# A hybrid SSD and attention block: short groups of transposes ahead of the quads of the gate and up products

## The chip, the cores and the metric

The kernel runs on one core of one Trainium2 chip. The metric is the time of the whole kernel on the device, in microseconds (us); lower is better.

## The reference

One layer of a streaming-encoder block in float32, for 1024 tokens of width 1024. A Mamba-2 SSD group (8 heads) and a stick-breaking attention group (8 heads) work side by side on one projection, then comes a SwiGLU channel mixer with 2816 hidden channels. Cut to the parts that matter here:

```python
h = rms_norm(x, pre_mix_gain)
proj = h @ w_in
z, xbc, dt_raw, q, k, v = split(proj)
y_ssd = ...   # convolution, SSD scan, gated, normed
y_sb = ...    # stick-breaking attention, normed
mix = concatenate([y_ssd, y_sb]) @ w_out
x = x + rms_norm(mix, post_mix_gain)

h = rms_norm(x, pre_ffn_gain)
f = (silu(h @ w_gate) * (h @ w_up)) @ w_down
x = x + rms_norm(f, post_ffn_gain)
```

## The kernel before

Every product is made from operands that are split into two parts: `hi` is the value rounded to float32r and `lo` is what is left of it. ScalarE makes `hi` and VectorE makes `lo` (`split`, L72 and L73), and three matmuls take the place of one: hi x hi, hi x lo, lo x hi (`mm3`, L76 to L78).

The program goes through these stages: the projection together with attention and SSD (to about 485 us), out_proj with its norms (to about 600 us, where the first products of gate and up already stand between its blocks), gate and up (to 1031 us), and down with the last norm.

Gate and up are multiplied as the seven products of Winograd's form of Strassen's product. The 22 tiles of hidden channels are taken in 11 pairs. For each pair p there is one quad for gate and one for up, and `quad(p, name)` is a generator that makes one of the seven products at a time, in the order of its right operands B11, B21, T2, T3, T1, T4, B22. `step(p)` takes the next product of gate's quad and then the same of up's quad, so PE gets gate 1, up 1, gate 2, up 2 and so on. A product is 4 x 3 = 12 matmuls of 128x512 into one bank of PSUM, and a pair of quads has 14 products, 168 matmuls. In the text below "a quad" means such a pair, and "the third quad" is p = 2. The eight banks are taken in a ring, four by gate (`pag`, `pbg`, `pcg`, `peg`) and four by up, so each quad gets the same bank for the same purpose. The bank `pa` holds the first product, goes on accumulating the second, and is then read by the Silu of `gate` (L1002).

Where the operands lie matters below. A tile pool is put on the left or on the right side of the on-chip memory. The right operands of gate and up (B11, B21, T2, T3 in pool `rpA`, T1, T4, B22 in pool `rpB`) lie on the left. The left operands (`flhi`, `fllo`, pool `fw`) lie on the right, except those of the first two products of the first quad (`eo`, in the e tiles of `fwA`), which lie on the left. In down both operands (`fohi`, `folo`) lie on the right. In out_proj W_out (`woh`, `wol`) lies on the right, and the other operand `yhl` too, but for the blocks 2 and 3, where `out_load` puts `yhl` on the left, in the places of T3.

The left operands are loaded, split and kept five steps ahead by `pump(1 + LOOK)`. In the last quad, the loop also starts the loads and splits of down (`unit`, `prep`).

The identity `ident` (128x128, float32, on the left) is used for the transposes that turn the normed rows in out_proj (L1061: 4 transposes for a half, 8 for a block). The clock of TensorE rises with use: the program makes 12 products of ones at its very start (L104).

Of the kernel before, what the change touches and what calls it, by code (L numbers as in the profile page):

```python
# [34 lines left out]
# what in_proj makes, in order; "ssd" from where on SSD's steps run beside the tiles  # L35
PLAN = ('qkv1', 'x0', 'x1', 'x2', 'x3', 'x4', 'x5', 'qkv2', 'x7', 'x6', 'ssd', 'qkv3', 'z0', 'z1', 'r0', 'z2', 'z3', 'wo', 'l1', 'o0')
# how far attention is where the other stream is 0, 1/8, .. 1 done
PACE = (-0.109, 0.104, 0.264, 0.337, 0.474, 0.601, 0.751, 0.876, 1.027)
A_ALL, F_ALL = 146.4, 259.0
SIDE = 1  # L40
WARM = 12
# [6 lines left out]
def tile_hybrid_block(  # L48
# [15 lines left out]
    """The rows of x and out run backwards in time (row s is token S-1-s), so that every  # L64
    running product over earlier tokens is a forward scan along the free axis."""
# [4 lines left out]
    def split(hi, lo, src):  # L70
        """hi + lo == src, hi and lo each exact in float32r."""
        A.copy(hi, src)  # L72
        V.tensor_tensor(lo, src, f32(hi), ALU.subtract)  # L73
# [6 lines left out]
    # ------------------------------------------------------------------ constants  # L80
# [20 lines left out]
    # TensorE's clock rises with use: products of ones while the first loads run  # L101
# [3 lines left out]
    # tri[s, l] = 1 where s >= l  # L105
    tri = const.tile([P, P], F32, name="tri")
    G.affine_select(tri, ones_f, [[-1, P]], ALU.is_ge, 0.0, base=0, channel_multiplier=1)
    # scan floor: 1 where the key is not strictly before the query, 0 elsewhere
# [3 lines left out]
    # column h is 1 on the 64 partitions of head h of a pair  # L112
# [11 lines left out]
    # DRAM scratch  # L124
# [5 lines left out]
    # means of squares and what they make 1 / rms: even heads, odd heads, SSD groups  # L130
# [8 lines left out]
    # ------------------------------------------------------------------ right side: x * gain and in_proj weights  # L139
# [4 lines left out]
    # the rows' 1 / rms scales columns here, so it is applied to what comes out of in_proj  # L144
# [13 lines left out]
    # sel16 sums the products of the two halves of w2  # L158
# [11 lines left out]
    # columns of w_in in the order of their use; each tile is loaded and split while the one before it  # L170
    # is multiplied
# [5 lines left out]
    def fetch_w(half=None):  # L177
        """The next column tile, or one half of it."""
        if cols:
            name, col = cols[0]  # L180
            w = w_tiles.setdefault(name, [])
            for dh in range(2) if half is None else (half,):
                w.append(load_w_half(col, name, dh))
            if len(w) == 2:
                cols.pop(0)
# [8 lines left out]
    # ------------------------------------------------------------------ pre-mix norm, first products  # L194
# [40 lines left out]
    # ------------------------------------------------------------------ left side: attention, conv and SSD work  # L235
# [20 lines left out]
    def qkv_tiles(j, st):  # L256
        """What takes q, k (each in its two parts) and v of a pair of heads out of PSUM, to DRAM."""

        def store(key, n, i, t):
            nc.sync.dma_start(qkv_d[j][key][i][:, 512 * n : 512 * n + 512], t)  # L260

        def two(key, n, src):
            hi, lo = [t2.tile([P, 512], F32R, tag="t2", name=key + x) for x in "hl"]
            split(hi, lo, src)
            store(key, n, 0, f32(hi))
            store(key, n, 1, f32(lo))

        def evac_q(n, ps, sl):
            two("q", n, ps)
            st["q"] = n == 1  # L270

        def evac_k(n, ps, sl):
            kr = t2.tile([P, 512], F32, tag="t2", name="kr")
            V.tensor_tensor(kr, ps, R_b[:, sl], ALU.mult)
            two("k", n, kr)
            st["k"] = n == 1

        def evac_v(n, ps, sl):
            vr = t2.tile([P, 512], F32, tag="t2", name="vr")
            V.tensor_tensor(vr, ps, R_b[:, sl], ALU.mult)  # L280
            if j == 0:
                v_first.append(vr)
            else:
                store("v", n, 0, vr)
            if n == 1:
                st["v"] = True

        return evac_q, evac_k, evac_v
# [7 lines left out]
    # ------------------------------------------------------------------ dt, decays  # L296
    def dt_stage():
# [18 lines left out]
        # softplus(x) = max(x, 0) + log1p(exp(-|x|)), log1p(e) = 2 atanh(e / (2 + e))  # L316
# [43 lines left out]
        # attention's sigmoids, which need these, wait for the last exponential: ScalarE changes its table once  # L360
# [4 lines left out]
    # ------------------------------------------------------------------ conv tiles  # L365
# [38 lines left out]
    # ------------------------------------------------------------------ SSD  # L404
# [76 lines left out]
    def mean_sq(src, sel, rows, n, cnt, ps=None, start=True, stop=True):  # L481
        """Means of squares over channels, to the rows of ss_d."""
# [32 lines left out]
    # ------------------------------------------------------------------ stick-breaking attention  # L515
    CH = {128: [128], 256: [256], 384: [384], 512: [512], 640: [384, 256], 768: [512, 256], 896: [512, 384], 1024: [512, 512]}

    def prep_head(j, st, h):
        """Keys over both halves of the partitions, the query's high part beside its low part."""
# [29 lines left out]
    def weigh(head, qb):  # L549
        """A key k weighs sigmoid(z_k) * prod_{q < i < k} sigmoid(-z_i)."""  # L550
# [20 lines left out]
    def turn(ws, g, jj):  # L571
        """Weights of 256 queries and 256 keys, keys to the partitions, split."""
# [27 lines left out]
    def attention(st):  # L600
        """All heads, as one stream of small steps: products with the values lag the transposes,
        the next queries' weights run ahead of them."""
# [53 lines left out]
    def merge(ga, gb):  # L656
        """Interleave attention with the other stream, as PACE has it."""
# [47 lines left out]
    # ------------------------------------------------------------------ out_proj: the products  # L705
    # position p of a block of 128 tokens: from here on the last rows come first
# [6 lines left out]
    def bank(name):  # L713
        tag = ("mm", "mm", "z", "z", "o", "px", "px", "px")[ring_i[0] % 8]
        ring_i[0] += 1
        return psum(tag, name)
# [4 lines left out]
    # the channels in the order of their use: attention's first, the SSD's second group last  # L721
    KO = (4, 5, 6, 7, 0, 1, 2, 3)

    def fetch_wo():
        """W_out's rows in the order of their use, and the places of their two parts."""
# [31 lines left out]
    def out_load(p, part):  # L757
        """A block of the mixed channels, scaled by their 1 / rms, split: all but the SSD's second
        group, that group, or all."""
# [89 lines left out]
    # ------------------------------------------------------------------ out_proj, post-mix norm, residual, pre-ffn norm  # L849
    # positions 0 .. 7 of a block of 128 tokens: from here on the last rows come first  # L850
# [3 lines left out]
    def row_rstd(ssq):  # L854
        """-2 (ssq / D + eps) ** -0.5 for [P, 2] partial sums; the gains it multiplies take in the -1 / 2."""
# [15 lines left out]
    # Gate and up as the seven products of Winograd's form of Strassen's product: blocks of 512  # L871
    # tokens, halves of d, and pairs of tiles of f. h2 is the right operand:
    #   [b11 b12; b21 b22], halves of d by halves of the tokens
# [13 lines left out]
    def product(ps, lop, rop, start):  # L887
        """ps = or += the product; a bank that was read goes on accumulating after that."""
        (ah, al), (bh, bl) = lop, rop
        for k in range(4):  # L890
            mm3(ps, ah[:, k, :], al[:, k, :], bh[:, k, :], bl[:, k, :], start and k == 0, k == 3, not start)
# [4 lines left out]
    def quad(p, name):  # L896
        """The 2 x 2 blocks of W^T h from seven products. c11 is left in PSUM."""
        tmp = lambda: gp.tile([P, 512], F32, tag="bt", name="c" + name, bufs=4)
        x = "gu".index(name)
        a = bank("pa" + name)  # L900
        product(a, lops[x], B11, True)
# [31 lines left out]
    def left_gen():  # L933
        """The left operands in the order of their use, gate and up in turn."""
# [51 lines left out]
    def step(p):  # L986
        """The next product of gate's and of up's quad p."""
# [8 lines left out]
    def gate(t):  # L996
        """A block of a from gate's and up's."""
# [8 lines left out]
    # which block of a the products make  # L1006
    where = {1: (0, 0), 4: (1, 1), 5: (1, 0), 6: (0, 1)}

    with es_o:
# [3 lines left out]
        def early_ops():  # L1013
            """The left operands of the first two products."""
# [35 lines left out]
        def out_tail(sb, t):  # L1050
# [20 lines left out]
            # T3 = b22 - b12, T2 = T3 + b11, T1 = b12 - b11, T4 = b21 - T2: its product enters with that sign  # L1071
# [50 lines left out]
        # not the ring's next banks: those hold what waits for the last norm  # L1122
# [7 lines left out]
    # ------------------------------------------------------------------ gate and up  # L1130
# [12 lines left out]
    # Down as seven products too: halves of the tokens, even and odd tiles of f, halves of d.  # L1143
    #   a: [a11 a12; a21 a22], tokens by f; w: [b11 b12; b21 b22], f by d
    # What stays on chip takes the places of what gate and up no longer need, in this order.
# [35 lines left out]
    def prep(i):  # L1181
        """The operands of a step, a product's part of one pair of tiles of f."""
# [60 lines left out]
    # ------------------------------------------------------------------ down, post-ffn norm, residual  # L1243
# [15 lines left out]
    def finish(b, halves, xr):  # L1259
        """halves: the block's two, times the gain."""  # L1260
# [76 lines left out]
def _layout(inputs):  # L1337
    """x backwards in time, plain and transposed; the small parameters side by side, a channel
    (of its tile of 128) to a partition; the large ones as they are."""
# [32 lines left out]
```

## Time and profile before

| | |
|---|---|
| median of 3 runs | 1249.93 us (1248.95 to 1252.76) |
| the profiled execution | span 1249.6 us, 0.3 us under the median |
| PE (matmul) busy | 1204.2 us, 96% |
| VectorE (DVE) busy | 932.1 us, 75% |
| ScalarE (ACT) busy | 587.7 us, 47% |
| GpSimd (POOL) busy | 92.1 us, 7% |
| mean granted TensorE clock | 0.989 |

The span is the time from the first to the last instruction of one profiled execution. Busy times are shares of the span. PE and PEld are the matmuls and the weight loads of TensorE, which overlap. A matmul is shown longer than the distance to the next one's start, because matmuls are pipelined, so the rate is read from the distance between starts. The granted clock is 1.00 at 2.4 GHz and 0.50 at 1.2 GHz.

### The profile page before, as it was taken

Reading aid. Unit: us, or ns where it says so; the run is one execution under the profiler, and the core shown is the slowest. Engines: PE = TensorE matmul, PEld = TensorE weight load, DVE = VectorE, ACT = ScalarE, POOL = GpSimd, SP = SyncE. Lnnn points to the kernel's source line nnn. Section 1 sums busy time; section 2 is a strip of 40 time slices with the busy share of each in tenths; the row PEclk is TensorE's granted clock in tenths of the full one; section 3 lists DMA queues with packets and bytes.
Section 4 is the critical chain, followed back from the end, with each engine's and each line's share of the span. In section 5 each row is a group of like instructions: output and inputs, shape, how many; then the busy total and the mean of one; then the engine's idle time right before and its main releaser. Section 6 shows DMA issues by size and latency. Waiting matters only on the chain.

```text
span 1249.6 us, 16320 instructions
## 1 busy us (share of the span) xinstructions
PE 1204.2 (96%) x5641; PEld 972.0 (78%) x5641; DVE 932.1 (75%) x1461; ACT 587.7 (47%) x1115; POOL 92.1 (7%) x232
## 2 busy tenths in 40 slices
PE   8998999999999998998799999999999999999997
PEld 7776778787887776787678888888888888888885
DVE  7478988778997887676897565566555558998777
ACT  7347655556655666444653332333233325444543
POOL 0041110010110100011200000000000000000000
PEclk9998999999999999999899999999999999999999
DMA  5693252445466326754872212312132198133336
GB/s 188 194 358 107 67 152 82 142 117 178 142 181 190 118 93 212 228 173 159 271 207 93 93 60 93 101 59 93 52 100 98 58 327 318 62 124 101 102 135 235
DMA packets 139882, 183.23 MB, mean 147 GB/s; under 512 B 10660, under 2 KB 94852, under 8 KB 139800
## 3 DMA queue, kind: packets, MB, share of 16 engines
q1 hardware_dynamic: 128544, 151.18, 38.3%
q0 software_dynamic: 7424, 25.17, 5.5%
q10 hardware_dynamic: 3832, 5.84, 1.3%
q8 instruction: 44, 0.72, 0.2%
q14 instruction: 38, 0.31, 0.1%
HBM read 132.23 MB, written 49.92 MB: 146 GB/s over the span
## 4 chain that ended last, share of the span: by engine, by line
PE 69%; DVE 14%; DMA 8%; issue 4%; ACT 4%; SPq 2%; DVEq 0%; ACTq 0%
PE pd L77 5%; PE pd L76 5%; PE pd L78 5%; DVE sn L567 3%; DMA Rb<-r_d 3%; PE o L590 2%; PE tp L578 2%; PE pj_x L76 2%; PE pj_x L78 2%; PE pcg L76 2%; PE pj_x L77 2%; PE pcu L76 2%; PE peg L76 2%; PE peu L76 2%; PE peu L77 2%
## 5 line engine op out<-in xcount | busy, mean ns | idle before, releaser
L72 ACT CAST flhi<-fraw 128x512 fp32r<-128x512 f32 x102 | 62.7, 622 | 174.1 <-PE pcg L77 37.0
L77 PE MATMUL pd<-folo,fohi 128*128 128x512 f32 x260 | 101.2, 389 | 0.0
L76 PE MATMUL pd<-fohi 128*128 128x512 f32 x260 | 101.2, 389 | 0.0
L78 PE MATMUL pd<-fohi,folo 128*128 128x512 f32 x260 | 101.1, 389 | 0.0
L567 DVE TENSOR_TENSOR_SCAN sn<-sn,smask 128x1024 f32<-128x1024 f32 (+3 forms) x64 | 87.4, 1366 | 17.7 <-ACT sn L563 17.7
L73 DVE TENSOR_TENSOR fllo<-fraw,flhi 128x512 fp32r<-128x512 f32 x102 | 69.6, 686 | 38.9 <-ACT flhi L72 38.5
L72 ACT CAST fohi<-rt 128x512 fp32r<-128x512 f32 x83 | 48.9, 618 | 51.2 <-PE pd L77 30.7
L563 ACT ACTIVATE sn<-zp,msc 128x512 f32<-128x512 f32 (+2 forms) x96 | 56.0, 585 | 34.3 <-PE zp L562 30.6
L582 ACT CAST wh<-tp 128x512 fp32r<-128x512 f32 (+1 forms) x80 | 42.7, 545 | 38.4 <-PE tp L578 37.9
L72 ACT CAST flhi<-fs 128x512 fp32r<-128x512 f32 x44 | 27.2, 622 | 70.4 <-PE peg L77 37.0
L73 DVE TENSOR_TENSOR folo<-rt,fohi 128x512 fp32r<-128x512 f32 x83 | 55.2, 694 | 6.4 <-ACT fohi L72 6.4
L583 DVE TENSOR_TENSOR wl<-tp,wh 128x512 fp32r<-128x512 f32 (+1 forms) x80 | 49.7, 628 | 10.8 <-ACT wh L582 10.3
L564 ACT ACTIVATE sp<-zp,msc 128x512 f32<-128x512 f32 (+2 forms) x96 | 55.8, 584 | 2.5 <-PE tp L578 2.5
L76 PEld LDWEIGHTS pd<-fohi 128*128 128x128 f32 x260 | 48.8, 188 | 10.3
L78 PEld LDWEIGHTS pd<-fohi,folo 128*128 128x128 f32 x260 | 48.8, 188 | 10.1
L77 PEld LDWEIGHTS pd<-folo,fohi 128*128 128x128 f32 x260 | 48.8, 188 | 10.1
L1004 POOL DMA_DIRECT2D a_d<-sg x44 | 23.7, 540 | 392.4 <-DVE sg L1003 392.4
L76 PE MATMUL pj_x<-hh,wh_x 128*128 128x512 f32 x128 | 52.5, 410 | 0.0
L578 PE MATMUL tp<-ident,sp 128*128 128x128 f32 x288 | 47.6, 276 | 5.0 <-DVE sp L568 4.5
L76 PE MATMUL po<-woh,yhl 128*128 128x512 f32 x128 | 51.0, 399 | 1.0 <-ACT yhl L72 1.0
L78 PE MATMUL po<-woh,yhl 128*128 128x512 f32 x128 | 51.0, 400 | 0.6 <-DVE yhl L73 0.5
L78 PE MATMUL pj_x<-hh,wl_x 128*128 128x512 f32 x128 | 51.1, 399 | 0.0
(422 smaller groups left out, 3479.4 us busy)
## 6 DMA issues: line engine op xcount, KB each, us to landing
ps<-a_d SPq DMA_DIRECT2D x55, 256.0 KB
fraw<-in_w_gate_dram SPq DMA_DIRECT2D x22, 512.0 KB
fraw<-in_w_up_dram SPq DMA_DIRECT2D x22, 512.0 KB
a_d<-sg POOLq DMA_DIRECT2D x44, 256.0 KB, 2.5
rt<-in_w_down_dram SPq DMA_DIRECT2D x33, 256.0 KB
rt<-a_d SPq DMA_DIRECT2D x22, 256.0 KB
ps<-in_w_down_dram SPq DMA_DIRECT2D x22, 256.0 KB
xt<-in_x_t_dram SPq DMA_DIRECT2D x8, 512.0 KB
```

The lines of the kernel that those rows point to most:

```text
L72: A.copy(hi, src)
L73: V.tensor_tensor(lo, src, f32(hi), ALU.subtract)
L76: T.matmul(ps, lhsT=ah, rhs=bh, start=start, stop=False, skip_group_check=more)
L77: T.matmul(ps, lhsT=ah, rhs=bl, start=False, stop=False, skip_group_check=more)
L78: T.matmul(ps, lhsT=al, rhs=bh, start=False, stop=stop, skip_group_check=more)
L563: A.activation(sn[:, 1 + off : 1 + off + cw_], zp[:, 0:cw_], AF.Sigmoid, scale=rqn[:, qb : qb + 1])
L564: A.activation(sp[:, off : off + cw_], zp[:, 0:cw_], AF.Sigmoid, scale=rqp[:, qb : qb + 1])
L567: V.tensor_tensor_scan(sn[:, 1 : 1 + W], sn[:, 1 : 1 + W], smask[:, 0:W], 1.0, ALU.mult, ALU.max)
L578: T.transpose(tp[:, P * i : P * i + P], ws[a][:, co : co + P], ident)
L582: A.copy(wh[:, 0:n_], tp[:, 0:n_])
L583: V.tensor_tensor(wl[:, 0:n_], tp[:, 0:n_], f32(wh[:, 0:n_]), ALU.subtract)
L590: T.matmul(o[:, 0:cw_], lhsT=vv[:, k, h, :], rhs=wt[:, c0 : c0 + cw_], start=(first and k == kb + 1 and wt is wh), stop=(last and k == kb ...
```

## The change

In gate's quads from the third on (p = 2 to 10), `SHORT[p]` transposes of the identity are issued into the bank `pa` ahead of the first product, in turn into its four 128x128 quarters. Up's quads have none. The product that follows starts the bank afresh, so nothing that the transposes write is read. The table has an entry for each quad: 8, 4, 2, 6, 8, 3, 5, 7 and 8 from p = 2 to p = 10.

```diff
 SIDE = 1
+SHORT = (0, 0, 8, 4, 2, 6, 8, 3, 5, 7, 8)
 WARM = 12
...
     def quad(p, name):
...
         tmp = lambda: gp.tile([P, 512], F32, tag="bt", name="c" + name, bufs=4)
         x = "gu".index(name)
         a = bank("pa" + name)
+
+        for i in range(SHORT[p] if name == "g" else 0):
+            T.transpose(a[:, P * (i % 4) : P * (i % 4) + P], ident, ident)
         product(a, lops[x], B11, True)
         p1 = e_tile(2 * x + p % 2, "p1" + name)
```

The new lines move the numbers of the lines behind them: by 1 from `SHORT` on and by 4 behind the new loop. No other instruction is added, removed or moved, on any engine or queue.

On PE's queue, where up's last product of a quad ends and gate's first of the next begins. Up's last products accumulate in `peu` with B22, gate's first is `pag` with B11. First the boundary between the second and the third quad, before:

```order
L76 MATMUL peu<-B22h,flhi 128x512
L77 MATMUL peu<-B22l,flhi 128x512
L78 MATMUL peu<-B22h,fllo 128x512
L76 MATMUL pag<-B11h,flhi 128x512
L77 MATMUL pag<-B11l,flhi 128x512
L78 MATMUL pag<-B11h,fllo 128x512
```

The same boundary on PE's queue, of the changed kernel:

```order
L77 MATMUL peu<-B22h,flhi 128x512
L78 MATMUL peu<-B22l,flhi 128x512
L79 MATMUL peu<-B22h,fllo 128x512
L904 MATMUL pag<-ident 128x128 x8
L77 MATMUL pag<-B11h,flhi 128x512
L78 MATMUL pag<-B11l,flhi 128x512
L79 MATMUL pag<-B11h,fllo 128x512
```

Eight matmuls with the identity as both operands stand between the two products. At the boundary between the fourth and the fifth quad (p = 4, where the table has 2) PE's queue of the changed kernel has:

```order
L77 MATMUL peu<-B22h,flhi 128x512
L78 MATMUL peu<-B22l,flhi 128x512
L79 MATMUL peu<-B22h,fllo 128x512
L904 MATMUL pag<-ident 128x128 x2
L77 MATMUL pag<-B11h,flhi 128x512
L78 MATMUL pag<-B11l,flhi 128x512
```

Here it is two, and what stands around them is as before.

## Rows read from the trace of the kernel before

**Rows 1.** The page: span, busy times of the engines, and of the 40 slices those of PE's busy share, in tenths.

```profile
span 1249.6 us, 16320 instructions
PE 1204.2 (96%) x5641; PEld 972.0 (78%) x5641; DVE 932.1 (75%) x1461; ACT 587.7 (47%) x1115; POOL 92.1 (7%) x232
...
PE   8998999999999998998799999999999999999997
```

**Rows 2.** The table of stretches: from and to in us, length, busy us (and instructions) of PE, PEld, DVE, ACT and POOL, granted clock, busy share of the DMA engines, GB/s. Third, fourth and last quad, then a stretch of down.

```profile
678.30:717.70 39.40, 39.40 (x171) 31.70 (x170) 22.80 (x36) 12.17 (x21) 2.16 (x4) 1.00 0.25 81
717.70:757.20 39.50, 39.50 (x171) 31.79 (x170) 23.64 (x37) 12.38 (x21) 2.16 (x4) 1.00 0.25 81
...
993.80:1033.20 39.40, 39.40 (x170) 31.73 (x170) 19.75 (x31) 12.07 (x20) 2.16 (x4) 1.00 0.83 298
...
1110.00:1150.00 40.00, 40.00 (x179) 33.10 (x178) 35.84 (x59) 19.54 (x35) 0.00 (x0) 1.00 0.24 80
```

**Rows 3.** The list of PE's waits from 599 to 1035 us (for whom, us in total, times, longest), complete, and then the timeline's rows of the longest and of the last: start, length, instruction, in brackets the idle time before it and what ended it.

```profile
PE pbg L76 <- ACT T2h L72: 3.3, 1, 3.3
PE pt L1061 <- DVE tm L1047: 2.7, 1, 2.7
PE pbu L76 <- ACT flhi L72: 0.7, 1, 0.7
PE pcg L76 <- DVE u3g L915: 0.5, 1, 0.5
...
617.84 0.50 PE L76 MATMUL pbg<-T2h,flhi 128*128 128x512 f32 x1 [3.26 <-ACT T2h L72]
...
639.12 0.47 PE L76 MATMUL pcg<-T4h,flhi 128*128 128x512 f32 x1 [0.48 <-DVE u3g L915]
```

**Rows 4.** The timeline of PE at the starts of the third, fourth, fifth and eleventh quad.

```profile
678.39 0.40 PE L76 MATMUL pag<-B11h,flhi 128*128 128x512 f32 x1
678.63 0.39 PE L77 MATMUL pag<-B11l,flhi 128*128 128x512 f32 x1
...
717.59 0.40 PE L76 MATMUL pag<-B11h,flhi 128*128 128x512 f32 x1
...
756.79 0.40 PE L76 MATMUL pag<-B11h,flhi 128*128 128x512 f32 x1
...
991.99 0.40 PE L76 MATMUL pag<-B11h,flhi 128*128 128x512 f32 x1
```

**Rows 5.** The view of the bank `pag`: the Silu that reads it; count, shortest, median and longest duration in ns, first and last start in us. Then the longest time that an engine sat idle before an instruction of this view by a wait (us, times): PE, ahead of 574.3 us.

```profile
L1002 ACT ACTIVATE sg<-pag x11: 592/592/599, 607.9 to 1000.9; 128x512 f32<-128x512 f32 x11
...
  DVE tm L1039: 3.8, 1
```

**Rows 6.** The view of the bank `pt`: the matmuls of out_proj's transposes, columns as in rows 5.

```profile
L1061 PE MATMUL pt<-ident,tm x64: 270/272/302, 521.6 to 614.1; 128*128 128x128 f32 x64
```

**Rows 7.** The timeline of PE: the start of out_proj's block 2, and two groups of eight transposes in a full stream of matmuls.

```profile
510.47 0.40 PE L76 MATMUL po<-woh,yhl 128*128 128x512 f32 x1
...
521.63 1.03 PE L1061 MATMUL pt<-ident,tm 128*128 128x128 f32 x8
522.42 0.48 PE L76 MATMUL po<-woh,yhl 128*128 128x512 f32 x1
522.74 0.40 PE L77 MATMUL po<-wol,yhl 128*128 128x512 f32 x1
...
598.60 1.03 PE L1061 MATMUL pt<-ident,tm 128*128 128x128 f32 x8
599.39 0.47 PE L76 MATMUL pag<-B11h,flhi 128*128 128x512 f32 x1
599.70 0.39 PE L77 MATMUL pag<-B11l,flhi 128*128 128x512 f32 x1
```

**Rows 8.** The timeline of PE: first matmuls of products whose distance gives the pace. `pau` with B21 and eo starts 12 matmuls ahead of 598.60; between the two rows of `pau` from 602 us on stand 24 starts, between those of `pd` 12.

```profile
595.87 0.39 PE L76 MATMUL pau<-B21h,eo 128*128 128x512 f32 x1
...
602.25 0.39 PE L76 MATMUL pau<-B11h,flhi 128*128 128x512 f32 x1
...
607.83 0.40 PE L76 MATMUL pau<-B21h,flhi 128*128 128x512 f32 x1
...
1031.19 0.39 PE L76 MATMUL pd<-fohi 128*128 128x512 f32 x1
...
1033.92 0.39 PE L76 MATMUL pd<-fohi 128*128 128x512 f32 x1
```

**Rows 9.** The table of stretches (columns as in rows 2) around three groups of eight transposes, and of two stretches at the lower clock.

```profile
521.00:523.00 2.00, 2.00 (x15) 1.73 (x14) 1.47 (x3) 1.40 (x4) 0.00 (x0) 1.00 0.98 276
...
557.50:559.20 1.70, 1.70 (x13) 1.48 (x13) 1.70 (x4) 0.02 (x1) 0.00 (x0) 1.00 0.88 266
...
598.40:600.20 1.80, 1.80 (x14) 1.58 (x13) 1.80 (x6) 1.78 (x5) 0.54 (x1) 1.00 1.07 366
...
574.30:577.40 3.10, 3.08 (x7) 2.48 (x8) 1.90 (x4) 1.93 (x7) 0.54 (x1) 0.50 0.27 80
618.40:625.00 6.60, 5.93 (x14) 4.68 (x15) 6.60 (x12) 4.14 (x8) 0.73 (x2) 0.50 0.62 197
```

**Rows 10.** The timeline of PE at the lower clock.

```profile
620.08 0.63 PE L78 MATMUL pbg<-T2h,fllo 128*128 128x512 f32 x1
620.51 0.63 PE L76 MATMUL pbg<-T2h,flhi 128*128 128x512 f32 x1
```

## The prediction

> **What bounds the kernel now.** I read the page first: the matmul engine PE is busy for 1204.2 of the 1249.6 us, and in the table of slices its digits are 9 all through the second half [rows 1]. That alone proves little, since a matmul's shown length (0.39 us) is longer than the distance to the next one. So I went to three closer views. The table of stretches puts PE at 39.40 of 39.40 us and the granted clock at 1.00 in the third quad as in the last, and PE still full in "down" behind it, while VectorE is busy for about 23 us of a quad and ScalarE for 12 [rows 2]. The list of PE's waits over all of gate and up has four rows, and in the timeline the last of these waits ends at 639.12 us, in the second quad [rows 3]. Behind that the starts are evenly spaced: gate's first product starts at 678.39, 717.59 and 756.79 us, and the eleventh quad's at 991.99 [rows 4]. (991.99 - 678.39) / 8 = 39.20 us for a quad, the same each time, with 168 matmuls in it: 233.3 ns from start to start. Nothing else than PE sets the pace from the third quad to nearly the end of the kernel, so whatever is put on PE's queue there is paid in full unless it changes the pace of what follows.
>
> **The change part by part.** It adds 8, 4, 2, 6, 8, 3, 5, 7 and 8 transposes, 51 in all, each a weight load and a 128x128 float32 matmul, and removes and reorders nothing. They stand between the last product of one quad and the first of the next. They write the bank that the product then starts afresh. That bank was last read by the Silu of the quad before: the last quad's starts 8.9 us behind the quad's first matmul (1000.9 and 991.99), which is 30 us ahead of the next quad [rows 4, 5]. So they wait for no reader, and the operand of the first product, for which the matmul behind them waits, is ready now with no gap [rows 3, 4]. So there is no stall that they could fill.
>
> The price of a transpose: the trace before has 64 of just this shape, which turn the normalized rows (L1061), each shown with 272 ns [rows 6]. They overlap: a group of eight takes 1.03 us from first start to last end, so (1.03 - 0.27) / 7 = 0.109 us lies between two starts. What a group costs is read from the two places where it stands in a full stream of matmuls [rows 7]. At 598.60 the first matmul behind it starts 0.79 us later, and the second 0.31 us after that instead of 0.23: 0.79 + 0.31 - 0.23 = 0.87 us. At 521.63 it is 0.79 + 0.32 - 0.23 = 0.88 us. For n transposes I take (n - 1) x 0.109 for the spacing, 0.03 from the last transpose to the matmul and 0.085 for that matmul's later successor. Over nine groups: 42 x 0.109 + 9 x 0.115 = 5.6 us. The nearest rows give the bounds: nothing below 51 x 0.109 = 5.5 us, and 51 x 0.272 = 13.9 us if no two overlapped, which both places speak against.
>
> The second term is the pace behind a group. The matmuls of this kernel run at more than one pace at the full clock [rows 8]. Where both operands lie on the same side of the on-chip memory it is 12 in 2.73 us (595.87 to 598.60: the e tiles and B21, both on the left; 1031.19 to 1033.92: "down", both on the right), 227 ns each. Where one lies left and the other right, as in gate and up from 599 us on (fl right, B and T left), it is slower, and there are two paces: 24 matmuls from 602.25 to 607.83 us, 232.5 ns each, and 233.3 ns from the third quad on. The two are separated by PE's last wait at 639.12 us and by nothing else: before it the first, behind it the second, for 390 us. So a break chooses the pace, and the pace then stays. Each group of transposes is such a break. Behind the groups at 521.63 and 598.60, the two that stand before products with operands on both sides, came the 232.5 pace. If all nine quads took it, each would gain 168 x 0.8 ns = 0.14 us, and all 1.3 us; if none did, nothing. Both precedents have eight transposes, and the change has eight in three quads only; I take half, 0.6 us.
>
> What follows is only moved. VectorE and ScalarE get later inputs by the same amount as PE gets later, and have some 16 and 27 us of slack in a quad. "Down" is paced by PE too, and its prepared operands keep their distance in PE's queue, so the 5 us go through to the end.
>
> Sum: 1249.6 (the profiled execution's span) + 5.6 - 0.6 = 1254.6 us. The median of the runs, 1249.93, stands 0.3 above that span, so for the runs 1254.9 us, 0.40% more. The bounds inside this case are 4.3 us (every quad on the faster of its two paces) and 5.6 us (none) of delay.
>
> **The clock.** The stretches around three groups of eight transposes, from 521 to 600 us, were all granted 1.00, that is 2.4 GHz; the two stretches at 0.50 (1.2 GHz) came where PE had stood idle for microseconds, 3.8 us before 574.3 and 3.3 us before 617.84 us [rows 3, 5, 9]. The Trainium skill, "TensorE: Matmul & The Clock Gate", Part 4, says that transposes do not count as PE work for the clock in the way matmuls do, so that the full clock does not engage for them. This is a rule against the change, and by it the clock might fall at a group; no group of eight in this trace shows that.
>
> **The rivals.**
> *A faster pace (ends faster than before).* A break might put the products of a quad on 227 ns as where both operands lie on one side. Price: 168 x 6.6 ns = 1.1 us a quad, against 0.62 us for an average group. It decides from five of nine quads on: 5.6 / 1.1. With all nine it is 1249.6 + 5.6 - 10.0 = 1245.2, for the runs 1245.5 us. For it: a break does choose a pace, and the counts differ. Against it: in the products with operands on both sides 227 ns did not come up, neither from 599 us on nor in the earlier ones of out_proj (48 matmuls from 510.47 to 521.63 us, 232.5 ns each), and at the change to "down" (1031.19 us) it came at once without any break [rows 7, 8]. Chance 0.07.
> *A slower pace.* A group could leave its quad on a worse rhythm. The nearest bound: if every distance were the longer of the two that alternate now (678.39 to 678.63 us, 0.24) [rows 4], a quad would lose 168 x 6.7 ns = 1.1 us and nine 10 us: 1265.5 us for the runs with the groups' own 5.6. Against it: not seen in any long stretch. Chance 0.05.
> *The clock falls at groups.* At 1.2 GHz a matmul starts every 427 ns (620.08 to 620.51 us, 0.43) [rows 9, 10]. A fall as long as the one from 574.3 us, 3.1 us, loses 3.1 x (1 - 233 / 427) = 1.4 us. At the three groups of eight: 4.2 us, 1259.1 us for the runs; at all nine 12.7 us, 1267.6. Chance 0.03.
> *No overlap of the transposes,* 13.9 us instead of 5.6: 1263.2 us. Both operands are the identity here, and another tile in the rows; I see no reason why this should matter. Chance 0.02.
> *Part of the delay is hidden,* by a wait that the views do not show or because a later stage catches up: under 3.75 us (0.3%) of delay. With PE at 100% in each stretch there is no place for it. Chance 0.03.
>
> **How the numbers follow.** The forecast has 0.80. Its own range is 1254.2 to 1255.5 us, which I widen by about 1 us on each side, as the three runs of before spread over 3.8 us: 1253 to 1256.5. The range for 8 in 10 also takes in mixtures of the forecast with one or two quads on another pace, and reaches from 1252.2 to 1257.5 us. About 0.3%, or 3.75 us, is what a measurement of this kernel tells from no change. Of the forecast's 0.80, I count 0.68 as slower by more than that (its lower end, 4.3 us, is only half a microsecond above) and 0.12 as within. The slower pace, clock and overlap rivals add 0.10 to slower; the hidden part adds 0.03 to the same, and a faster pace in only some quads 0.02. Faster by over 0.3% takes nearly all nine quads: 0.05, and 0.02 for what no row shows. Slower 0.78, same 0.16, faster 0.06 after rounding.
>
> **What the profile after would show.** Nine groups of PE rows with ident twice, before gate's first product; starts within a group 0.109 us apart; 0.3 us from the first matmul behind a group to its second. A quad then lasts 39.20 us, or 39.06 on the 232.5 pace, plus 0.109 us for each transpose: 40.07 with eight, 39.4 with two. The clock stays 1.00 from the third quad on, "down" keeps 12 matmuls in 2.73 us, and PE gets no new wait. The prediction is wrong if quads with the transposes taken off differ from 39.06 to 39.20 us, if matmuls behind a group keep a start distance below 230 ns or above 235 ns for long, or if the end does not move with PE.

## The result and the profile after

The changed kernel takes 1255.17 us (median of 6 runs, 1253.74 to 1259.04) against 1249.44 us of before (median of 6 runs, 1246.5 to 1252.76). The ratio is 1.0042, with a 95% interval of 1.0026 to 1.0058: 0.4% slower, 5.2 us by the ratio. The prediction was 1254.9 us, 0.40% slower.

The profiled execution of the changed kernel has a span of 1257.3 us and a time of its own of 1259.04 us, the longest of the six; in each of the six runs the time lies 1.7 to 1.8 us above the span. The page's span and busy times, to be read against [rows 1]:

```profile
span 1257.3 us, 16422 instructions
...
PE 1212.9 (96%) x5692; PEld 980.2 (78%) x5692; DVE 932.1 (74%) x1461; ACT 587.0 (47%) x1115; POOL 92.1 (7%) x232
```

PE has 51 matmuls and 51 weight loads more, and nothing else has changed in number. The 7.7 us between the two spans are not all the change's: the third quad starts at 681.50 us here and at 678.39 before [rows 4], 3.1 us that lie ahead of the first added instruction. The table of stretches for the third, the ninth and the last quad, columns as in [rows 2]:

```profile
681.50:721.40 39.90, 39.90 (x177) 32.48 (x176) 23.23 (x37) 12.07 (x20) 2.16 (x4) 1.00 0.26 80
919.10:958.80 39.70, 39.70 (x174) 32.04 (x173) 23.02 (x37) 12.10 (x20) 2.16 (x4) 1.00 0.26 80
998.80:1038.70 39.90, 39.90 (x177) 32.52 (x176) 19.54 (x30) 12.06 (x20) 2.16 (x4) 1.00 0.80 276
```

As before, PE is full and the granted clock is 1.00. The view of the added line gives the duration of one (shortest, median, longest in ns), and the timeline shows a group of eight and the group of five with the first matmuls behind them, which answer to [rows 6, 7]:

```profile
L904 PE MATMUL pag<-ident x51: 270/272/273, 681.5 to 999.6; 128*128 128x128 f32 x51
...
681.50 1.04 PE L904 MATMUL pag<-ident 128*128 128x128 f32 x8
682.29 0.47 PE L77 MATMUL pag<-B11h,flhi 128*128 128x512 f32 x1
682.61 0.39 PE L78 MATMUL pag<-B11l,flhi 128*128 128x512 f32 x1
...
919.11 0.71 PE L904 MATMUL pag<-ident 128*128 128x128 f32 x5
919.58 0.48 PE L77 MATMUL pag<-B11h,flhi 128*128 128x512 f32 x1
919.89 0.39 PE L78 MATMUL pag<-B11l,flhi 128*128 128x512 f32 x1
```

The eight take 0.79 us to the first matmul and that takes 0.32 to the next: the very numbers of [rows 7]. The starts of the other groups, and the start of down:

```profile
721.41 0.60 PE L904 MATMUL pag<-ident 128*128 128x128 f32 x4
760.88 0.38 PE L904 MATMUL pag<-ident 128*128 128x128 f32 x2
800.14 0.82 PE L904 MATMUL pag<-ident 128*128 128x128 f32 x6
839.82 1.03 PE L904 MATMUL pag<-ident 128*128 128x128 f32 x8
879.74 0.49 PE L904 MATMUL pag<-ident 128*128 128x128 f32 x3
...
958.86 0.93 PE L904 MATMUL pag<-ident 128*128 128x128 f32 x7
998.81 1.03 PE L904 MATMUL pag<-ident 128*128 128x128 f32 x8
1038.71 0.39 PE L77 MATMUL pd<-fohi 128*128 128x512 f32 x1
```

A quad lasts from one start to the next. With 0.109 us taken off for each transpose:

| quad | transposes | lasts us | without them | pace of its 168 matmuls |
|---|---|---|---|---|
| 3rd | 8 | 39.91 | 39.03 | 232.4 ns |
| 4th | 4 | 39.47 | 39.04 | 232.4 ns |
| 5th | 2 | 39.26 | 39.04 | 232.4 ns |
| 6th | 6 | 39.68 | 39.03 | 232.4 ns |
| 7th | 8 | 39.92 | 39.05 | 232.4 ns |
| 8th | 3 | 39.37 | 39.04 | 232.4 ns |
| 9th | 5 | 39.75 | 39.20 | 233.3 ns |
| 10th | 7 | 39.95 | 39.19 | 233.3 ns |
| 11th | 8 | 39.90 | 39.03 | 232.4 ns |

The nine quads together take 1038.71 - 681.50 = 357.2 us, against 1031.19 - 678.39 = 352.8 before [rows 4, 8]: 4.4 us more. From the start of down to the end it is 218.6 us here and 218.4 before. So in these two profiles the transposes cost 5.6 us and the faster of the two paces in seven quads gave 1.2 back. The pace in the last column is what is left of a quad, divided by 168; it comes out at one of two values, so the table fits the price of 0.109 us with one choice between two values, 0.16 us apart, for each quad.

### The profile page after: what moved, and what is told of

Read it like the earlier page. It is cut to its first block, busy times and chain, and to the rows that moved or that the text cites. A ratio compares the mean times of both kernels' runs of the same rounds, so it can differ in the third digit from the quotient of the medians.

```text
span 1257.3 us, 16422 instructions
## 1 busy us (share of the span) xinstructions
PE 1212.9 (96%) x5692; PEld 980.2 (78%) x5692; DVE 932.1 (74%) x1461; ACT 587.0 (47%) x1115; POOL 92.1 (7%) x232
## 4 chain that ended last, share of the span: by engine, by line
PE 70%; DVE 13%; DMA 7%; ACT 4%; issue 4%; SPq 1%; POOL 0%; DVEq 0%; ACTq 0%; POOLq 0%
PE pd L78 5%; PE pd L77 5%; PE pd L79 5%; DVE sn L568 3%; PE pcg L77 2%; PE pcg L78 2%; PE tp L579 2%; DMA Rb<-r_d 2%; PE o L591 2%; PE pj_x L77 2%; PE pcg L79 2%; PE pj_x L79 2%; PE pj_x L78 2%; PE peg L77 2%; PE peu L79 2%
## 5 line engine op out<-in xcount | busy, mean ns | idle before, releaser
L584 DVE TENSOR_TENSOR wl<-tp,wh 128x512 fp32r<-128x512 f32 (+1 forms) x80 | 49.7, 628 | 10.7 <-ACT wh L583 10.2
L78 PEld LDWEIGHTS pd<-folo,fohi 128*128 128x128 f32 x260 | 48.8, 188 | 10.3 <-DVE folo L74 0.2
L79 PEld LDWEIGHTS pd<-fohi,folo 128*128 128x128 f32 x260 | 48.8, 188 | 10.1
L77 PEld LDWEIGHTS pd<-fohi 128*128 128x128 f32 x260 | 48.8, 188 | 10.1
```

The lines of the kernel that those rows point to most:

```text
L77: T.matmul(ps, lhsT=ah, rhs=bh, start=start, stop=False, skip_group_check=more)
L78: T.matmul(ps, lhsT=ah, rhs=bl, start=False, stop=False, skip_group_check=more)
L79: T.matmul(ps, lhsT=al, rhs=bh, start=False, stop=stop, skip_group_check=more)
L584: V.tensor_tensor(wl[:, 0:n_], tp[:, 0:n_], f32(wh[:, 0:n_]), ALU.subtract)
```

## The experiments

The theory has two parts. A transpose costs 0.109 us wherever PE is full, and nothing where PE waits. And a matmul's pace depends on whether both operands lie on one side of the memory, while breaks only choose between two nearly equal paces where they do not. The rivals: the price lies in the break and not in the transposes; the count decides the pace; any break could bring the 227 ns pace, whatever the side; transposes pull the clock down.

The differences shown of the first three runs are against the changed kernel, the others against the kernel before or, where the text says so, against another run; `...` marks what is left out.

**Twice as many transposes.**

```diff
-SHORT = (0, 0, 8, 4, 2, 6, 8, 3, 5, 7, 8)
+SHORT = (0, 0, 16, 8, 4, 12, 16, 6, 10, 14, 16)
```

> Twice as many transposes in each group: 16, 8, 4, 12, 16, 6, 10, 14, 16, 102 in all. My theory is a price of 0.109 us for each transpose, paid in full since PE has no gap: 102 x 0.109 = 11.1 us, less at most 1.4 us if all quads take the faster of the two paces, so 9.7 to 11.1 us over before, a ratio of 1.0078 to 1.0089. Rival: the price lies in the break, once for each group, and a longer group costs no more: as the change itself, a ratio of about 1.004. Rival: a longer group of transposes lets the clock fall: stretches granted under 1.00 behind the groups of 16, and over 12 us.

Measured: 1260.52 us, ratio 1.0099 [1.0082, 1.0116]. The start of its third to sixth quad and of down, and the table's stretch from 676 to 718 us, which holds the third quad:

```profile
676.09 1.91 PE L904 MATMUL pag<-ident 128*128 128x128 f32 x16
716.87 1.03 PE L904 MATMUL pag<-ident 128*128 128x128 f32 x8
756.93 0.60 PE L904 MATMUL pag<-ident 128*128 128x128 f32 x4
796.56 1.47 PE L904 MATMUL pag<-ident 128*128 128x128 f32 x12
...
1039.19 0.39 PE L77 MATMUL pd<-fohi 128*128 128x512 f32 x1
...
676.00:718.00 42.00, 42.00 (x196) 34.44 (x194) 24.31 (x39) 12.68 (x21) 2.16 (x4) 1.00 0.23 76
```

The nine quads take 1039.19 - 676.09 = 363.1 us, 10.3 more than before, inside the expected 9.7 to 11.1. The measured ratio lies above the expected 1.0078 to 1.0089, but its interval reaches down to 1.0082, that is 10.2 us. The price is for each transpose and not for the break. The third quad with its 16 lasts 40.78 us, 39.03 without them; the fourth with 8 lasts 40.06, or 39.19. So here a group of eight left the slower of the two paces, while all three of the change left the faster. With groups of 16 the clock stayed at 1.00.

**Five in each quad.**

```diff
-SHORT = (0, 0, 8, 4, 2, 6, 8, 3, 5, 7, 8)
+SHORT = (0, 0, 5, 5, 5, 5, 5, 5, 5, 5, 5)
```

> Five transposes in each of the nine quads, 45 in all. What is open is what decides the pace behind a group: in the profile of the change the groups of 5 and 7 were followed by 233.3 ns from start to start, those of 8, 4, 2, 6, 8, 3 and 8 by 232.4. If the count decides, all nine quads run at 233.3 ns: 39.20 + 5 x 0.109 = 39.74 us each, 357.7 us for the nine. If a break picks one of the two paces by what went before it, some quads take 39.04 + 0.55 = 39.59 us and some 39.74. In both the delay against nine quads of 39.20 us lies between 3.5 and 4.9 us.

Measured: 1251.49 us, one run. The first three groups:

```profile
674.72 0.71 PE L904 MATMUL pag<-ident 128*128 128x128 f32 x5
714.46 0.71 PE L904 MATMUL pag<-ident 128*128 128x128 f32 x5
754.05 0.71 PE L904 MATMUL pag<-ident 128*128 128x128 f32 x5
```

The third quad lasts 39.74 us and the fourth 39.59: the same count, both paces. Seven of the nine quads took the faster one, and the nine together are 3.8 us longer than before's. The count alone does not decide.

**One in each quad.**

```diff
-SHORT = (0, 0, 8, 4, 2, 6, 8, 3, 5, 7, 8)
+SHORT = (0, 0, 1, 1, 1, 1, 1, 1, 1, 1, 1)
```

> One transpose ahead of each of the nine quads, the smallest break. My theory: price 0.12 us each, 1.0 us in all, and behind each break one of the two paces, 39.04 or 39.20 us for the 168 matmuls; so each quad 39.15 to 39.32 us, and the nine together 352.4 to 353.9 us against 352.8 (nine at 39.20) or 351.4 us (nine at 39.04). Rival: the last transposes and the first matmul of any group cost more than a transpose, say 0.3 us a group, 2.7 us in all.

Measured: 1249.30 us, one run. The starts of two quads that follow each other:

```profile
715.65 0.27 PE L904 MATMUL pag<-ident 128*128 128x128 f32 x1
...
754.80 0.27 PE L904 MATMUL pag<-ident 128*128 128x128 f32 x1
```

39.15 us, as expected, and eight of the nine quads so; the nine together last 352.5 us. One transpose costs 0.11 us, so a break has no price of its own worth speaking of.

**Transposes where PE waits.**

```diff
         b = bank("pb" + name)
+        for i in range(28 if p == 0 and name == "g" else 0):
+            T.transpose(b[:, P * (i % 4) : P * (i % 4) + P], ident, ident)
         product(b, lops[x], T2, True)
```

> No transposes ahead of the quads. Instead one group of 28 transposes stands ahead of the first quad's product with T2, into its bank, where PE waits 3.3 us for that operand. My theory: transposes cost only where PE is full. 28 x 0.109 = 3.05 us lie inside the wait, the first matmul with T2 starts as long after T2's split as before, and the quads from the third on stay at 39.20 or 39.04 us. Rival: a group delays what follows it by its own length wherever it stands: 3 us later. It also tells what transposes do for the clock: before, the clock fell to 0.50 for 6.6 us right behind this wait. If transposes count as use like matmuls do, the fall is shorter or absent, up to 6.6 x (1 - 233 / 427) = 3.0 us gained; if they do not count, it falls as before.

Measured: 1249.00 us, one run. Its timeline between the last of out_proj's transposes and the first product with T2, and, from the table, the stretch from 605 to 625 us:

```profile
611.32 0.60 PE L1063 MATMUL pt<-ident,tm 128*128 128x128 f32 x4
...
612.00 3.22 PE L909 MATMUL pbg<-ident 128*128 128x128 f32 x28
615.42 0.50 PE L76 MATMUL pbg<-T2h,flhi 128*128 128x512 f32 x1 [0.20 <-ACT T2h L72]
...
605.00:625.00 20.00, 17.34 (x92) 14.05 (x91) 18.35 (x33) 11.73 (x22) 3.69 (x7) 1.00 0.71 239
```

From out_proj's last group to the product with T2 it is 615.42 - 611.32 = 4.10 us. Before, the product started at 617.84 us [rows 3], 4.10 us behind that group, too:

```profile
613.74 0.60 PE L1061 MATMUL pt<-ident,tm 128*128 128x128 f32 x4
```

Twenty-eight transposes, 3 us of PE, cost nothing there; the wait of 3.3 us has become one of 0.2. From the second quad's first matmul to the third quad's it is 78.9 us, against 79.0 before. The same stretch of before was granted 0.84 on average:

```profile
605.00:625.00 20.00, 13.29 (x48) 10.05 (x48) 17.00 (x32) 11.02 (x20) 3.77 (x7) 0.84 0.63 225
```

With the transposes it was 1.00. The wait ahead of out_proj's transposes happened to be shorter in this run, too (1.7 us against 2.7). That alone does not explain it: in the profiles of the runs with five and with one in each quad, with twice as many, with each product's own operand and with the change on top of the left operands, that wait was 1.7 to 1.8 us as well, and the stretch was granted 0.83 to 0.91. The clock fell later here, to 0.50 at 636.5 us, behind a wait of 2.2 us ahead of the product with T4.

**Matmuls in the same place.**

```diff
         b = bank("pb" + name)
+        for i in range(13 if p == 0 and name == "g" else 0):
+            T.matmul(b, lhsT=B21[0][:, i % 4, 0:P], rhs=B11[0][:, i % 4, :], start=True, stop=True)
         product(b, lops[x], T2, True)
```

> As the run with 28 transposes in the wait ahead of the first product with T2, but with 13 float32r matmuls of 128x512 (B21 by B11, both ready) in their place, 13 x 0.227 = 2.95 us, whose result the product writes over. With the transposes the clock stayed at 1.00 where it had fallen to 0.50 before. If transposes and matmuls count alike for the clock, the stretch from 605 to 625 us is granted 1.00 here too; if the transposes' run was luck of the moment, it may fall. The time up to the third quad's start, 79.0 us from the second quad's first matmul before, changes by less than 1.5 us, since VectorE's chain of splits paces it (PE waited for T2, u3 and T1 there with the transposes, too).

Measured: 1253.96 us, one run. The stretch from 605 to 625 us, and the one from 617.2 us to the next fall of the clock:

```profile
605.00:625.00 20.00, 16.53 (x69) 13.03 (x68) 16.30 (x30) 10.17 (x21) 4.32 (x8) 0.91 0.60 218
617.20:640.90 23.70, 20.73 (x87) 15.97 (x87) 22.32 (x37) 14.09 (x25) 2.16 (x4) 1.00 0.89 252
```

The clock fell at 613.7 us, within the wait of 2.7 us ahead of out_proj's transposes and so ahead of the added matmuls; the mean of 0.91 is this fall's. Behind the product with T2, which starts at 620.00 us, it did not fall until 641.0 us, again behind a wait of 2.2 us ahead of the product with T4.

All twelve profiles together say more than this run alone. In the ten in which nothing was added in this place, PE waited 2.8 to 3.3 us for T2, and the clock stood at 0.50 at the latest 2.0 us behind the end of that wait. In the two with 28 transposes or 13 matmuls there it did not fall behind the product with T2. This speaks for the transposes keeping the clock up there as the matmuls do. It is one execution of each, so it is not proved, and whether transposes count in full for the clock is not shown.

From the second quad's first matmul to the third quad's it was 80.5 us, 1.5 us longer than before, at the edge of what was expected.

**Both operands on the left.** In this kernel the first 128 columns of B11 are the left operand of every product from the third quad on.

```diff
         (ah, al), (bh, bl) = lop, rop
+        if on_left[0]:
+            ah, al = [t[:, :, 0:P] for t in B11]
...
+        on_left[0] = p > 1
```

> No transposes. In gate and up from the third quad on, each matmul takes its left operand from the first 128 columns of B11 (left side of the on-chip memory) instead of from fl (right side), so that both operands lie on the left; the products of these quads are other numbers than the reference wants. Loads, splits and everything else stay. My theory: the pace depends on whether both operands lie on one side. Then a matmul starts every 226.7 ns in these quads instead of every 233.3, a quad takes 38.08 us instead of 39.20, and nine save 10.1 us: a ratio of 0.992. Rival: the side does not matter and the pace is picked by breaks alone: 232.4 or 233.3 ns and a ratio of 0.999 to 1.000.

Measured: 1249.09 us, ratio 1.0 [0.9987, 1.0014]. The time is the rival's, but the profile is not. The timeline at the start of the last quad and of down, with what PE waited for, the list's row of what ScalarE waited for there, and the loads that SyncE's queue issues then:

```profile
983.43 0.39 PE L76 MATMUL pag<-B11h 128*128 128x512 f32 x1
...
1028.85 0.80 PE L76 MATMUL pd<-fohi 128*128 128x512 f32 x1 [7.18 <-ACT fohi L72]
...
ACT fohi L72 <- DMA rt<-a_d: 7.3, 1, 7.3
...
1021.52 6.40 SPq L1163 DMA_DIRECT2D rt<-a_d  x8
```

The last quad starts 8.6 us earlier than before (983.43 against 991.99 [rows 4]). Then PE waits 7.2 us for down's first operand, ScalarE waits for that operand's load, and the load goes into the place of B11, which this experiment kept busy to the end: the last quad's last matmul starts at 1021.29 us and the loads at 1021.52, where before the first of them started at 997.59. The clock also fell in that wait, to 0.50 from 1024.7 to 1035.0 us. The experiment took its own gain back.

**Each product's own right operand as its left one.** The difference is against the run before it.

```diff
-            ah, al = [t[:, :, 0:P] for t in B11]
+            ah, al = [t[:, :, 0:P] for t in rop]
```

> No transposes. As the run with B11 as left operand, but each product from the third quad on takes the first 128 columns of its own right operand as left operand, so that no tile is held longer than before. (The products are again other numbers than the reference wants.) There the nine quads ran at 38.08 to 38.43 us but the eleventh ended with a wait of 7.2 us for down's first operand, whose load into the place of B11 waited until B11 was free. My theory: that wait came from B11 alone, and here the gain gets through: 38.08 us a quad, 227 ns between starts in all seven products, 9 x 1.12 = 10.1 us, a ratio of 0.992. Rival: down's first operands cannot come 10 us earlier anyway (its loads and splits take the last quad's time), PE waits at the start of down, and the ratio stays above 0.996. Rival on the pace: what counts is a nearness of addresses that B11 had and T1 or B22 do not have; then some of the seven products stay at 232 or more.

Measured: 1241.00 us, ratio 0.9944 [0.9925, 0.9964]. The starts of the fourth and the last quad and of down:

```profile
711.64 0.39 PE L76 MATMUL pag<-B11h 128*128 128x512 f32 x1
...
978.20 0.39 PE L76 MATMUL pag<-B11h 128*128 128x512 f32 x1
1016.29 0.39 PE L76 MATMUL pd<-fohi 128*128 128x512 f32 x1
```

(978.20 - 711.64) / 7 = 38.08 us for a quad, 226.7 ns between starts, and 38.09 for the last. There is no wait at the start of down, and the gain gets through in this profile: its nine quads are 10.1 us shorter than before's. It is that of the fastest of the six runs (1236.30 to 1245.04 us). The ratio, 7.0 us with an interval of 4.5 to 9.4, falls short of the expected 0.992; where the other runs lost the rest is not shown. All seven products run at the faster pace, so a special place of B11 was not the reason.

**A kernel with the left operands on the left.** The result is the reference's again: the left operands from the third quad on take the e tiles, and what these held goes to the right, where the f ring shrinks. In the last quad three of down's steps are prepared ahead instead of four (the last two lines).

```diff
+    def r_tile(i, name):
+        return fw.tile([P, 512], F32, tag=f"r{i}", name=name, bufs=1)
...
-        ... name="f" + name + x, bufs=10) for x in ("hi", "lo")]
+        ... name="f" + name + x, bufs=6) for x in ("hi", "lo")]
+    def left_pair(name):
+        k = 2 * (n_left[0] % 4)
+        n_left[0] += 1
+        return [e_tile(k + i, "f" + name + x, F32R) for i, x in enumerate(("hi", "lo"))]
...
-                    hi, lo = [... for t in pair("l")]
+                    hi, lo = [... for t in (pair if p < 2 else left_pair)("l")]
...
-        pump(1 + LOOK)
+        pump(3 if p < 2 else 2)
...
-            if n_pairs[0] % 12 < 10:
+            if i % 6 < 3:
                 o.append(pair("o"))
+            elif i % 6 < 5:
+                o.append(left_pair("o"))
...
-                if i > 3:
+                if 3 < i < 7:
```

> No transposes, and the result is the reference's. From the third quad on the left operands of gate and up go to the e tiles on the left (a ring of 4 pairs, so two steps are kept ahead instead of five), and what the e tiles held goes to the right in place of 8 of the 20 buffers of the f ring. In down, steps take both operands on one side: three of six steps from the f ring, two from the e tiles, one from dp. My theory: both operands of each product from the third quad on lie on the left, a matmul starts every 227 ns, a quad takes 38.1 us, and about 10 us are saved, as with the products' own operands, where the ratio was 0.9944 [0.9925, 0.9964] and nine quads took 38.08 us each: a ratio of 0.991 to 0.995, if two steps ahead are enough. Rival: with only two steps ahead PE waits for its operands in gate and up, and the gain is lost there. Rival: down, with VectorE nearly full at its start, cannot begin 10 us earlier and waits.

Measured: 1238.81 us (5 runs, 1236.86 to 1240.28), ratio 0.9908 [0.9893, 0.9924]. The same starts, and the list of PE's waits from 590 us to the end, complete:

```profile
713.91 0.39 PE L76 MATMUL pag<-B11h,flhi 128*128 128x512 f32 x1
...
980.47 0.39 PE L76 MATMUL pag<-B11h,flhi 128*128 128x512 f32 x1
1018.55 0.39 PE L76 MATMUL pd<-fohi 128*128 128x512 f32 x1
...
PE pbg L76 <- ACT T2h L72: 3.3, 1, 3.3
PE pt L1072 <- DVE tm L1058: 2.6, 1, 2.6
PE pbg L77 <- DVE T2l L73: 0.4, 1, 0.4
```

38.08 us a quad, and all three waits, one at out_proj's transposes and two at T2, lie ahead of the third quad. Two steps ahead are enough. The ratio is just below the expected 0.991 to 0.995. This version is 0.9% faster than before and 1.3% faster than the change.

**The same without the left.** The control of the kernel above, against which the difference is shown: all the edits but the place of gate's and up's left operands.

```diff
-                    hi, lo = [... for t in (pair if p < 2 else left_pair)("l")]
+                    hi, lo = [... for t in pair("l")]
```

> The control to the kernel with the left operands on the left: all its other edits (two steps kept ahead, the e tiles' later contents on the right, the mix of rings in down), but gate's and up's left operands stay in the f ring on the right, of six pairs. My theory: the side alone made the difference, so a quad takes 39.04 or 39.20 us again and the ratio to before is 0.998 to 1.001. Rival: part of the gain came from the other edits (fewer loads ahead, another order of splits); then quads stay at 39 us but the ratio is below 0.996.

Measured: 1248.64 us, ratio 0.9997 [0.998, 1.0014]. Fourth quad, last quad and down start at:

```profile
714.65 0.39 PE L76 MATMUL pag<-B11h,flhi 128*128 128x512 f32 x1
...
987.93 0.39 PE L76 MATMUL pag<-B11h,flhi 128*128 128x512 f32 x1
1026.97 0.39 PE L76 MATMUL pd<-fohi 128*128 128x512 f32 x1
```

39.04 us a quad, and no gain. The place alone made the difference. The kernel before shows the same with other operands: in out_proj, where W_out lies on the right throughout, the matmuls of blocks 2 and 3, with `yhl` on the left, start every 232.4 ns, and those of the other blocks, with `yhl` on the right, every 226.7 ns once some ten matmuls have passed behind their transposes.

**The change on top of the left operands.** The difference is against the kernel with the left operands on the left.

```diff
+SHORT = (0, 0, 8, 4, 2, 6, 8, 3, 5, 7, 8)
...
+        for i in range(SHORT[p] if name == "g" else 0):
+            T.transpose(a[:, P * (i % 4) : P * (i % 4) + P], ident, ident)
```

> The kernel with both operands on the left, and the change's 51 transposes on top. My theory: the price of a transpose is the same, 0.109 us, and with both operands on one side there is one pace alone, which breaks don't alter: quads of 38.08 + 0.109 n us, 38.95 with eight, 38.30 with two. 5.6 us more than without the transposes: a ratio to before of about 0.9953 (0.9908 + 5.6 / 1250). Rival: a break picks the pace here too, and some quads run at 39 us or more.

Measured: 1243.80 us, ratio 0.9959 [0.9941, 0.9976], 0.4% above the kernel without the transposes by the medians and 0.5% by the ratios, as expected. The fourth to sixth quad start at:

```profile
714.25 0.60 PE L907 MATMUL pag<-ident 128*128 128x128 f32 x4
752.80 0.38 PE L907 MATMUL pag<-ident 128*128 128x128 f32 x2
791.13 0.81 PE L907 MATMUL pag<-ident 128*128 128x128 f32 x6
```

38.55 and 38.33 us, that is 38.11 without four and two transposes. The nine quads together are 5.9 us longer than without the transposes. All nine come back to 226.7 ns, within some ten matmuls behind a group.

## Why the prediction was right, point by point

**PE alone sets the pace, so what is put on its queue is paid in full.** Right. PE is busy for the whole of each quad after as before, and from the third quad on the list of PE's waits has one row alone, 0.3 us at 1239 us, near the end of down. Transposes in a place where PE waits cost nothing, in one run.

**0.109 us for a transpose, 5.6 us for 51.** Right. Quads with 2 to 8 transposes agree with it to 0.02 us, as do groups of 1 and of 16. The rival without overlap (13.9 us) is out.

**A break chooses the pace, 0.6 us of gain.** Half right. There are two paces, a break chooses between them, and the count does not decide it: 1, 4, 5 and 8 were each followed by either. Taking half of the gain was a guess. Seven of nine quads took the faster, 1.2 us of the 1.4 that were there against the profile of before. That is measured against the profile of one execution, as the forecast's term was. In the control run and in the run with transposes in the wait, which have no breaks at the quads, all nine quads ran at 39.04 us, and in the run with matmuls in the wait at 39.20, as in the profile of before. Which pace such a run holds is settled at the last wait ahead of the third quad, and a wait moves it both ways: from 233.3 to 232.4 ns in the run with transposes in the wait, from 232.4 to 233.3 in the run with matmuls and before (all three at the product with T4), and from 233.3 to 232.4 in the control (at the products with T1).

These are four kernels with one profile each; that executions of one kernel differ in this way was not measured. If they do, the change gains less here over many runs than the 1.2 us that the two profiles show. The measured 5.2 us (1.0026 to 1.0058, that is 3.2 to 7.2) can't tell 4.4 from 5.6, so it does not confirm this term, and that the median (1255.17) came within 0.3 us of the forecast (1254.9) is in part luck. What sets the pace at a break was not found.

**The 227 ns pace belongs to operands on one side, and breaks don't bring it.** Right, and shown from both sides: with both operands on the left, 226.7 ns in all seven products, with or without breaks; in the control, with the left operands back on the right, 232.4. Whether the side as such counts, or the distance of the addresses, was not tried.

**The clock stays up.** Right for the groups in full streams: 1.00 in every quad, with groups up to 16. The Trainium skill, "TensorE: Matmul & The Clock Gate", Part 4, has transposes not count as work for the clock; by that rule a fall was a rival here, and no run of this case shows one behind a group. In the run with 28 of them in the wait ahead of T2, too, the clock stayed up where the profiles without added work there have it at 0.50.

**The base of the sum.** The forecast put the profiled span 0.3 us under the median and added that. In the six runs of the changed kernel a time lies 1.7 to 1.8 us above its span. The forecast was saved by being, in effect, the median plus a difference. The wait that ends at 639.12 us stands ahead of the first quad's product with T4, not in the second quad, as the forecast put it; nothing hung on that.

## What to carry to other kernels

Where one engine is full without a gap, the price of added work is its distance from start to start, not its shown length, and it can be read from the same instruction elsewhere in the trace. Even starts tell more than a busy share: matmuls of one shape that run at 227 ns in one stage and at 233 in another, both at the full clock, point to where their operands lie, and putting both on one side gave this kernel 0.9%. An experiment that holds a tile longer than the kernel does can hide a gain behind a load into that tile's place, so the profile tells more there than the time.

## What the runs showed of the hardware

A 128x512 float32r matmul with a new weight load each time started every 226.7 ns where both operands lay on the left or both on the right, and every 232.4 or 233.3 ns where one lay on each side. The two slower paces are lasting rhythms: one held for 390 us without a change, and a break of a single transpose is enough to move from one to the other.
